# State outputs behind the chain, the output stage in two parts, and priority for three kinds of VectorE instruction, in an RWKV-7 and differential-attention trunk

## The chip, the cores and the metric

The kernel runs on one core of a Trainium2 chip. The metric is the device time of one execution in microseconds, lower is better. Engines are called as the profile calls them: PE is TensorE's matrix multiplier (PEld its weight loads), DVE is VectorE, ACT is ScalarE, POOL is GpSimd, SP is SyncE. L174 is line 174 of the kernel before.

## What is computed

Two layers over 2048 tokens of width 1024 in float32. The first is the one that matters here: a projection of the normalised input, RWKV-7 time mixing over 12 heads of 64 (a state matrix per head that is updated token by token), beside a small cross attention into 256 memory tokens. The second layer is differential attention. Cut to the recurrence:

```python
def step(state, inp):
    r_t, w_t, k_t, v_t, kk_t, a_t = inp
    sa = jnp.einsum('bhvk,bhk->bhv', state, -kk_t)
    state = (state * w_t[:, :, None, :]
             + sa[..., None] * (kk_t * a_t)[:, :, None, :]
             + v_t[..., None] * k_t[:, :, None, :])
    y_t = jnp.einsum('bhvk,bhk->bhv', state, r_t)
    return state, y_t
...
y = ((y - mean) * lax.rsqrt(var + LNX_EPS)).reshape(B, S, BR_W) * lnx_w + lnx_b
bonus = jnp.sum(r * k * r_k, axis=-1, keepdims=True) * v
return y + bonus.reshape(B, S, BR_W)
```

## The kernel before

Layer A is cut into 24 steps: two halves of the sequence, in each half six pairs of heads, for each pair two blocks of 512 tokens. A pair's weights serve both of its blocks. A step handles a block in chunks of 64 tokens: within a chunk the recurrence becomes small matrix products, and from chunk to chunk the state goes through a chain of eight links.

The methods of class Step are the stages of one step. p1 projects k, r and v (pj, three passes of 24 products at L174, 24 products for each) and mixes each with the token before (mix: an ACT copy with a scale, two DVE additions, and a copy of the last column, named carry, for the next block). Between k and r it takes a sum of squares per head over TensorE (pss, L335), which needs the mixed k (kx), its product kk on DVE and a square rn on ACT. p2 makes the Gram products (pg) and transposes; p3 and p3b invert the 64x64 triangular matrices of a chunk (DVE's recurrence itmp and Ti, transposes T and TT, and products inv, invz, invr on TensorE); p4 makes the products that turn a chunk into one affine map (atp, nvp, txp, mrp, and ch at L530). gate projects the SiLU gate (24 more pj).

p4b is the chain: for each of the eight chunks one product into ch (L541) reads the state before the chunk and one ACT instruction scales it into the next state (L542, S, and sb for the last). A link is this pair. The outputs yp take 32 products: 16 that need no state (L550) and 16 that read a chunk's state (L555, two for a chunk); in the profile each such product stands as two records. p5 is the output stage: statistics over a head (bn_stats, a few 128x8 operations on DVE, and two on ACT), two 128x512 operations on DVE (L574, L575), four transposes py on TensorE (L578), an ACT copy with the norm's weights, an addition, and the product with the gate on POOL, which also issues the store.

The kernel is written with tile pools; a scheduler sets each engine's order from priorities, which follow the order in which the code is written, and from its own estimate of when an instruction is ready. The loop over steps lets p2 and p3 of the next step stand ahead of p4b and p5 of this one, with p1 and gate of later steps as filler. All projections of layer A take turns in three PSUM banks (tag pj); the rest of layer A in three others, and ch in two of its own. On the engines the order is fixed then, and each engine runs its queue in that order.

A stretch, below, is the time from the first Gram product (pg) of one step to that of the next; there are 24. In stretch 3 and on, it holds the chain of the step before, the gate and the k projection of later steps, then pss, then 48 products for r and v. Weight halves are loaded by SP (wraw), copied by ACT (wh, L122) and split by POOL (wl, L123) once a pair, in turn with the projections that read the old ones.

Of the kernel before, what the change touches and what calls it, by code (L numbers as in the profile page):

```python
# [11 lines left out]
ALU = mybir.AluOpType  # L12
# [13 lines left out]
TB = 512  # L26
NC = TB // C
NJ = NC // 2
# [8 lines left out]
BIG = float(2.0 ** 60)  # L37
# [22 lines left out]
def hybrid_kernel(ctx, tc, S, HALF, x, mem, pv, cv, dist, postn, w_out, w_mkv, a_w, w2, a2, w_kv, b_w, out):  # L60
# [3 lines left out]
    mm = nc.tensor.matmul  # L64
    V = nc.vector
# [143 lines left out]
    def layer_a(ph):  # L209
# [17 lines left out]
        carry = pa.tile([P, 19], F32, name="carry")  # L227
# [25 lines left out]
        def PS(shape, name, tag="gm", bufs=3):  # L253
            if tag == "pj":
                return ppj.tile(shape, F32, name=name, tag="pj", bufs=3)
            return pps.tile(shape, F32, name=name, tag=tag, bufs=bufs)
# [17 lines left out]
        def mix(ps, col, o):  # L274
            m = pc("mu", col)
            A.activation(o, ps, AF.Copy, scale=omu[:, col:col + 1])
            V.scalar_tensor_tensor(out=o[:, 1:TB], in0=ps[:, 0:TB - 1], scalar=m, in1=o[:, 1:TB], op0=ALU.mult, op1=ALU.add)
            V.scalar_tensor_tensor(out=o[:, 0:1], in0=carry[:, col:col + 1], scalar=m, in1=o[:, 0:1], op0=ALU.mult, op1=ALU.add)
            V.tensor_copy(out=carry[:, col:col + 1], in_=ps[:, TB - 1:TB])

        def gate_silu(ps, g, eng=G_):
            A.activation(g, ps, AF.Copy)  # L282
            e = W([P, TB], "e_sil")
            A.activation(e, g, AF.Exp, scale=-1.0)
            V.tensor_scalar(out=e, in0=e, scalar1=BIG, scalar2=None, op0=ALU.min)
            A.activation(e, e, AF.Ln, bias=1.0)
            A.activation(e, e, AF.Exp, scale=-1.0)
            eng.tensor_tensor(out=g, in0=g, in1=e, op=ALU.mult)
            return g
# [13 lines left out]
        class Step:  # L303
# [5 lines left out]
            def p1(self):  # L309
                p, h, th, ws = self.p, self.h, self.th, self.ws  # L310
# [4 lines left out]
                for i, e in enumerate((cum[:, :, 1:65], asg.rearrange("p (c t) -> p c t", t=C))):  # L315
                    pl = PS([P, TB], "lr", "pj")
                    mm(pl, lhsT=lora[:, i], rhs=th[i], start=True, stop=False)
                    mm(pl, lhsT=lora[:, 2 + i], rhs=th[i], start=False, stop=True)
                    A.activation(e, pl.rearrange("p (c t) -> p c t", t=C), AF.Exp, bias=nwa[:, i * 6 + p:i * 6 + p + 1], scale=-1.0)
                    V.tensor_scalar(out=e, in0=e, scalar1=BIG, scalar2=None, op0=ALU.min)  # L320
                    A.activation(e, e, AF.Ln, bias=1.0)
                    A.activation(e, e, AF.Exp, scale=-1.0)
                kx = W([P, TB], "kx")
# [209 lines left out]
            def p4b(self):  # L533

                Gm, UV, PC, ch, MT, RT = self.Gm, self.UV, self.PC, self.ch, self.MT, self.RT
                hcs = (slice(0, 64), slice(64, 128))
                b = self.t0 // TB
                S = T([P, NC, C], "S", 1)
                st = [sb[self.p][:, b % 2]] + [S[:, c] for c in range(1, NC)] + [sb[self.p][:, 1 - b % 2]]
                for c in range(NC):  # L540
                    mm(ch[:, c, :], lhsT=MT[:, c, :], rhs=st[c], start=False, stop=True, skip_group_check=True)  # L541
                    A.activation(st[c + 1], ch[:, c, :], AF.Copy, scale=PC[:, c:c + 1])  # L542
                ys = self.ys = T([P, NJ, 2, C], "ys", 1)

                py = [PS([P, NJ, C], "yp") for hh in range(2)]
                for hh in range(2):
                    for j in range(NJ):
                        for e in range(2):
                            rr = hcs[e]
                            mm(py[hh][rr, j, :], lhsT=Gm[:, e, j, hh, rr], rhs=UV[:, 2 * j + e, hcs[hh]], start=j == 0, stop=False, skip_group_check=True)  # L550
                for j in range(NJ):
                    for e in range(2):
                        for hh in range(2):
                            c, rr = 2 * j + e, hcs[e]
                            mm(py[hh][rr, j, :], lhsT=RT[hcs[hh], c, :], rhs=st[c][hcs[hh]], start=False, stop=True, skip_group_check=True)  # L555
                for hh in range(2):
                    A.activation(ys[:, :, hh], py[hh], AF.Copy)

            def p5(self):
                p, ys, sil = self.p, self.ys, self.sil  # L560
                bs = T([P, 8, 6], "bs", 1)
                y8 = ys.rearrange("p j h v -> p (j h) v")
                for i in range(8):
# [9 lines left out]
                A.activation(sm[:, 3], sm[:, 3], AF.Exp, scale=-0.5)  # L573
                V.tensor_tensor(out=y8, in0=y8, in1=sm[:, 0, :, None].broadcast_to([P, 8, 64]), op=ALU.subtract)  # L574
                V.tensor_tensor(out=y8, in0=y8, in1=sm[:, 3, :, None].broadcast_to([P, 8, 64]), op=ALU.mult)  # L575
                py = PS([P, NJ, P], "py")
                for j in range(NJ):
                    nc.tensor.transpose(py[:, j, :], ys[:, j].rearrange("p h v -> p (h v)"), ident)  # L578
# [114 lines left out]
        for i in range(n):  # L693
# [10 lines left out]
            steps[i].p5()  # L704
            if i + 1 < n:
                steps[i + 1].p3b()
                steps[i + 1].p4()
            if i + 2 <= n:
                filler(i + 2)
            if i == n - 2:  # L710
# [613 lines left out]
```

## Time and profile before

| | |
|---|---|
| median of three runs | 3177.18 us (3177.15 to 3179.72) |
| the profiled execution's own time | 3178.13 us |
| its span in the trace | 3176.3 us |
| PE busy | 2965.9 us, 93% of the span |
| mean granted clock of TensorE | 0.970 |

The profile is of one execution. Its time is 0.95 us above the median and 1.8 us above its span. Busy shares are shares of the span; a busy PE is not one at its peak, since matmuls are pipelined and their ends are modelled. Layer A with its 24 stretches runs from 72 to some 1490 us of the span.

### The profile page before, as it was taken

What the parts mean: (1) busy time and instruction counts of PE and PEld (TensorE: products, weight loads), DVE (VectorE), ACT (ScalarE), POOL (GpSimd) and SP (SyncE); (2) the same over time, 40 slices, a digit from 0 to 9 for tenths busy, and PEclk for the clock granted to TensorE, in tenths of its full rate; (3) what the DMA queues carried; (4) which work ended last, traced back from release to release, by engine and by line L of the source; (5) the groups of instructions that cost most, each with busy time, mean ns of one, the idle gap of its engine ahead of it and who ended that gap; (6) DMA issues with size and microseconds to landing.
All of it is one profiled execution on the core that took longest, in us unless ns stands there. A gap on an engine that the chain in (4) does not pass through costs nothing.

```text
span 3176.3 us, 57448 instructions
## 1 busy us (share of the span) xinstructions
PE 2965.9 (93%) x22378; PEld 2401.6 (76%) x22378; DVE 1792.0 (56%) x4728; ACT 1508.2 (47%) x3318; POOL 873.6 (28%) x936
## 2 busy tenths in 40 slices
PE   6889999998789999998899999999999999998999
PEld 4667777776667777777677798898887787786777
DVE  6566767655656676764465311101108888887554
ACT  5535454444444544444455422313216777776343
POOL 3133433442134334431000222412312223222100
PEclk8999999998789999999999999999999999999999
DMA  3211000122110001103554523423454556533453
GB/s 118 80 30 36 28 23 26 35 77 79 36 33 28 23 26 33 38 25 86 164 145 126 155 80 99 118 83 87 117 158 110 114 112 120 116 80 108 121 156 115
DMA packets 266160, 265.45 MB, mean 84 GB/s; under 512 B 16832, under 2 KB 206656, under 8 KB 265760
## 3 DMA queue, kind: packets, MB, share of 16 engines
q1 hardware_dynamic: 237760, 195.31, 21.0%
q0 software_dynamic: 28128, 66.46, 10.3%
q8 instruction: 176, 2.88, 0.4%
q14 instruction: 96, 0.79, 0.1%
HBM read 180.45 MB, written 81.26 MB: 82 GB/s over the span
## 4 chain that ended last, share of the span: by engine, by line
PE 71%; DVE 13%; ACT 8%; issue 3%; DMA 3%; POOL 1%; SPq 1%; ACTq 0%; DVEq 0%; POOLq 0%
PE pj L174 28%; PE po L866 10%; PE o L1179 5%; PE vps L1042 4%; PE s L1138 3%; PE s L1139 2%; PE tr L1169 2%; DMA wraw<-in_a_w 2%; PE inv L446 2%; PE yp L555 1%; PE ch L541 1%; PE mo L805 1%; DVE E L1141 1%; PE mpt L798 1%; PE pss L335 1%
## 5 line engine op out<-in xcount | busy, mean ns | idle before, releaser
L174 PE MATMUL pj<-hhi,wh 128*128 128x512 f32 x928 | 396.3, 427 | 7.8 <-ACT sil L282 2.6
L174 PE MATMUL pj<-hhi,wl 128*128 128x512 f32 x928 | 379.4, 409 | 1.3 <-POOL wl L123 1.3
L174 PE MATMUL pj<-hlo,wh 128*128 128x512 f32 x928 | 373.9, 403 | 0.2 <-DVE hlo L149 0.2
L123 POOL TENSOR_TENSOR wl<-wraw,wh 128x512 fp32r<-128x512 f32 x168 | 220.0, 1320 | 431.5 <-ACT wh L122 378.0
L1141 DVE CUSTOM_DVE_ANT_0 E<-s,dist 128x512 f32<-128x512 f32 (+1 forms) x480 | 276.0, 604 | 35.2 <-PE s L1139 29.0
L174 PE MATMUL pj<-bh,wh 128*128 128x512 f32 x672 | 262.4, 391 | 0.0
L174 PE MATMUL pj<-bh,wl 128*128 128x512 f32 x672 | 262.3, 390 | 0.0
L174 PE MATMUL pj<-bl,wh 128*128 128x512 f32 x672 | 262.2, 390 | 0.0
L1146 ACT ACTIVATE E<-E,nm 128x1920 f32<-128x1920 f32 (+7 forms) x192 | 229.4, 1199 | 59.0 <-DVE nm L1144 58.6
L174 PEld LDWEIGHTS pj<-hhi,wh 128*128 128x128 f32 x928 | 179.2, 193 | 64.7 <-ACT sil L282 8.9
L122 ACT ACTIVATE wh<-wraw 128x512 fp32r<-128x512 f32 x168 | 105.2, 627 | 231.3 <-PE pj L174 143.6
L1179 PE MATMUL o<-th,vs 128*128 128x256 f32 (+1 forms) x864 | 210.9, 376 | 2.4 <-ACT th L1172 0.9
L174 PEld LDWEIGHTS pj<-hlo,wh 128*128 128x128 f32 x928 | 179.7, 194 | 41.7 <-issue 6.8
L174 PEld LDWEIGHTS pj<-hhi,wl 128*128 128x128 f32 x928 | 178.6, 192 | 42.0 <-POOL wl L123 2.2
L1138 PE MATMUL s<-ks,qd 128*128 128x512 f32 (+1 forms) x480 | 205.7, 432 | 2.2 <-DVE mx L1141 1.2
L1179 PEld LDWEIGHTS o<-th,vs 128*128 128x128 f32 x864 | 153.9, 189 | 38.5 <-ACT th L1172 19.2
L1139 PE MATMUL s<-ks,qd 128*128 128x512 f32 (+1 forms) x480 | 176.2, 373 | 0.0
L174 PEld LDWEIGHTS pj<-bh,wh 128*128 128x128 f32 x672 | 126.6, 188 | 26.3 <-DVE ot L877 0.3
L174 PEld LDWEIGHTS pj<-bh,wl 128*128 128x128 f32 x672 | 126.5, 188 | 26.3
L174 PEld LDWEIGHTS pj<-bl,wh 128*128 128x128 f32 x672 | 126.5, 188 | 25.9
L764 POOL DMA_DIRECT2D mq<-mq x64 | 33.3, 526 | 376.0 <-PE ms L783 368.3
L1172 ACT ACTIVATE th<-tr 128x512 f32<-128x512 f32 (+1 forms) x216 | 113.2, 568 | 44.2 <-PE tr L1169 43.8
(416 smaller groups left out, 7112.1 us busy)
## 6 DMA issues: line engine op xcount, KB each, us to landing
wraw<-in_a_w SPq DMA_DIRECT2D x126, 256.0 KB, 2.9
qd<-qd_d POOLq DMA_DIRECT2D x48, 512.0 KB, 7.0
mq<-mq POOLq DMA_DIRECT2D x64, 256.0 KB, 4.3
ks<-ks_d POOLq DMA_DIRECT2D x24, 512.0 KB, 7.2
yr<-y_dram SPq DMA_DIRECT2D x31, 384.0 KB, 5.0
xt<-in_x SPq DMA_DIRECT2D x16, 512.0 KB, 5.3
x_dram<-ot SPq DMA_DIRECT2D x16, 512.0 KB, 4.2
wraw<-in_b_w SPq DMA_DIRECT2D x32, 256.0 KB, 3.1
```

What stands on the lines that cost most here:

```text
L122: A.activation(hi[:, ks], raw, AF.Copy)
L123: eng.tensor_tensor(out=lo[:, ks], in0=raw, in1=hi[:, ks].bitcast(F32), op=ALU.subtract)
L174: mm(ps, lhsT=w[a_][:, k, wcol], rhs=h[b_][:, k, tsl], start=n == 0, stop=n == 3 * KT - 1)
L446: mm(pb[rows, j, hh, :], lhsT=lt[rows, j, hh, :], rhs=rt_[rows, j, hh, :], start=True, stop=True)
L866: mm(po[hf], lhsT=a_[:, k, :], rhs=b_[hf][:, k, :], start=k == i == 0, stop=k == KT - 1 and i == 2)
L1042: mm(ps[:, t, :], lhsT=hT[b][a_][:, k, tsl], rhs=w[b_][:, k, :], start=n == 0, stop=n == 3 * KT - 1)
L1138: mm(ps[:, f:f + w_], lhsT=qd[:, 0, c, qs], rhs=k_[:, c, 0:w_], start=True, stop=False)
L1139: mm(ps[:, f:f + w_], lhsT=qd[:, 1, c, qs], rhs=k_[:, c, 0:w_], start=False, stop=True)
L1141: V.tensor_tensor_reduce(out=e[:, kb * 512:kb * 512 + w], in0=ps[:, 0:w], in1=dt_[:, u0:u0 + w], scale=-SLOPES[h], scalar=3.0e38, op0=ALU. ...
L1146: A.activation(E[c][:, 0:nk], E[c][:, 0:nk], AF.Exp, bias=nm[:, c:c + 1], scale=-1.0, accum_out=nm[:, 2 + c:3 + c])
L1172: A.activation(th[:, 0:w], ps[:, 0:w], AF.Copy)
L1179: mm(po[:, oc], lhsT=vs[kt // 4][:, kt % 4, :], rhs=th[:, rc], start=n == 0, stop=n >= nmm - 2, skip_group_check=True)
```

## The change

Four edits, all of them in layer A. In p4b the 16 outputs that read a state (L555) get an edge that puts them behind the chain's last product in TensorE's order. p5 is cut in two: what follows L575, from the transposes py on, becomes p5b, which is called after the next step's p3b and ahead of its p4 (for the last step at the end). In mix, the three DVE instructions that read the projection's bank, and in p1 and gate_silu the min on DVE, are traced with high priority for the scheduler. No instruction is added or taken away: the count of each kind on each engine is the same.

```diff
         def mix(ps, col, o):
             m = pc("mu", col)
             A.activation(o, ps, AF.Copy, scale=omu[:, col:col + 1])
-            V.scalar_tensor_tensor(out=o[:, 1:TB], in0=ps[:, 0:TB - 1], scalar=m, in1=o[:, 1:TB], op0=ALU.mult, op1=ALU.add)
-            V.scalar_tensor_tensor(out=o[:, 0:1], in0=carry[:, col:col + 1], scalar=m, in1=o[:, 0:1], op0=ALU.mult, op1=ALU.add)
-            V.tensor_copy(out=carry[:, col:col + 1], in_=ps[:, TB - 1:TB])
+            with tc.high_priority():
+                V.scalar_tensor_tensor(out=o[:, 1:TB], in0=ps[:, 0:TB - 1], scalar=m, in1=o[:, 1:TB], op0=ALU.mult, op1=ALU.add)
+                V.scalar_tensor_tensor(out=o[:, 0:1], in0=carry[:, col:col + 1], scalar=m, in1=o[:, 0:1], op0=ALU.mult, op1=ALU.add)
+                V.tensor_copy(out=carry[:, col:col + 1], in_=ps[:, TB - 1:TB])
...
-            V.tensor_scalar(out=e, in0=e, scalar1=BIG, scalar2=None, op0=ALU.min)
+            with tc.high_priority():
+                V.tensor_scalar(out=e, in0=e, scalar1=BIG, scalar2=None, op0=ALU.min)
...
                 for c in range(NC):
-                    mm(ch[:, c, :], lhsT=MT[:, c, :], rhs=st[c], start=False, stop=True, skip_group_check=True)
+                    last = mm(ch[:, c, :], lhsT=MT[:, c, :], rhs=st[c], start=False, stop=True, skip_group_check=True)
...
-                for j in range(NJ):
-                    for e in range(2):
-                        for hh in range(2):
-                            c, rr = 2 * j + e, hcs[e]
-                            mm(py[hh][rr, j, :], lhsT=RT[hcs[hh], c, :], rhs=st[c][hcs[hh]], start=False, stop=True, skip_group_check=True)
+                with tc.issue_after(last.ins):
+                    for j in range(NJ):
+                        for e in range(2):
+                            for hh in range(2):
+                                c, rr = 2 * j + e, hcs[e]
+                                mm(py[hh][rr, j, :], lhsT=RT[hcs[hh], c, :], rhs=st[c][hcs[hh]], start=False, stop=True, skip_group_check=True)
...
+            def p5b(self):
+                p, ys, sil = self.p, self.ys, self.sil
                 py = PS([P, NJ, P], "py")
...
             if i + 1 < n:
                 steps[i + 1].p3b()
+                if True:
+                    steps[i].p5b()
                 steps[i + 1].p4()
+            if False or i + 1 == n:
+                steps[i].p5b()
```

What the scheduler makes of it shows at three places. First TensorE at a chain, in a stretch in the middle of the first half. Names are out<-in; ch<-sb and ch<-S are the chain's products, yp<-UV the outputs without a state, yp<-sb and yp<-S those with one, pj projections. Before:

```order
L385 MATMUL pvt<-cvt,vx 128x128 x4
L541 MATMUL ch<-sb_122,MT 128x64
L550 MATMUL yp<-UV,Gm 64x64 x16
L555 MATMUL yp<-sb_122,RT 64x64 x2
L541 MATMUL ch<-S,MT 128x64
L555 MATMUL yp<-S,RT 64x64 x2
L174 MATMUL pj<-hhi,wh 128x512
L174 MATMUL pj<-hlo,wh 128x512
L541 MATMUL ch<-S,MT 128x64
```

The same place in the changed kernel (its lines stand 2 to 7 lower):

```order
L388 MATMUL pvt<-cvt,vx 128x128 x4
L544 MATMUL ch<-sb_122,MT 128x64
L553 MATMUL yp<-UV,Gm 64x64 x16
L174 MATMUL pj<-hhi,wh 128x512
L544 MATMUL ch<-S,MT 128x64
L174 MATMUL pj<-hlo,wh 128x512
L174 MATMUL pj<-hhi,wl 128x512
L544 MATMUL ch<-S,MT 128x64
```

The outputs with a state are gone from between the links; they stand in one run of 16 behind the eighth. Between two links there are two projections now, where one and two took turns.

Second, TensorE ahead of pss, in every second stretch. Before, the chunk products ch<-UV are followed by pss at once:

```order
L519 MATMUL mrp<-BKT,Wn 64x64
L520 MATMUL mrp<-Gm,Wn 64x64
L530 MATMUL ch<-UV,BKT 64x64 x16
L335 MATMUL pss<-rn,cvt 128x512
L174 MATMUL pj<-hhi,wh 128x512
```

In the changed kernel nine products of the k projection and the first three links of the next step's chain come in between (the last of the nine and the links):

```order
L174 MATMUL pj<-hhi,wh 128x512
L174 MATMUL pj<-hlo,wh 128x512
L174 MATMUL pj<-hhi,wl 128x512
L544 MATMUL ch<-sb_122,MT 128x64
L544 MATMUL ch<-S,MT 128x64 x2
L338 MATMUL pss<-rn,cvt 128x512
```

The k projection ends there right ahead of the links and of pss, which needs what is made from it. It did end ahead of invr, a good deal earlier. Stretches 3, 5, 7, 9, 15, 17, 19, 21 and 23 have this form, and stretch 11 with two links; stretch 13 has it in both kernels, and stretch 14 had four links there before and none now. The stretches between (4, 6, 8 and so on) begin with what is left of the chain, five links.

Third, ACT at the same place in the changed kernel; kx is the mixed k, Pt and cum belong to the decay, S are the links' scalings, rn the square for pss:

```order
L122 ACTIVATE wh<-wraw 128x512
L276 ACTIVATE kx<-pj,omu 128x512
L331 ACTIVATE Pt<-cum 128x520
L545 ACTIVATE S<-ch,PC 128x64
L332 ACTIVATE cum<-cum 128x520
L545 ACTIVATE S<-ch,PC 128x64
L122 ACTIVATE wh<-wraw 128x512
L336 ACTIVATE rn<-kk 128x512
```

The two scalings and both weight halves stand among the instructions that pss waits for; before, no S stood between kx and rn in these stretches.

## Rows read from the trace of the kernel before

**Rows 1.** The page, part 1: busy time, share of the span, instructions.

```profile
PE 2965.9 (93%) x22378; PEld 2401.6 (76%) x22378; DVE 1792.0 (56%) x4728; ACT 1508.2 (47%) x3318; POOL 873.6 (28%) x936
```

**Rows 2.** Windows: length, busy PE, PEld, DVE, ACT, POOL, granted clock, DMA.

```profile
480.50:531.60 51.10, 47.06 (x539) 37.70 (x538) 33.48 (x93) 23.70 (x52) 19.96 (x20) 1.00 0.10 30
531.60:581.10 49.50, 46.96 (x537) 37.42 (x536) 36.35 (x93) 24.25 (x53) 20.19 (x20) 1.00 0.09 28
581.10:633.60 52.50, 48.58 (x536) 38.73 (x536) 33.59 (x93) 23.80 (x52) 19.89 (x20) 0.97 0.11 32
905.30:966.10 60.80, 52.81 (x541) 42.07 (x540) 36.55 (x93) 24.30 (x53) 19.12 (x19) 0.89 0.07 22
966.10:1014.90 48.80, 45.68 (x531) 35.82 (x530) 35.43 (x93) 22.72 (x49) 19.35 (x20) 1.00 0.09 28
```

**Rows 3.** Waits of PE from 431 to 581.1 us: total, times, longest.

```profile
PE py L578 <- DVE ys L575: 3.0, 3, 1.3
PE pg L371 <- DVE carry L279: 1.8, 2, 1.2
PE txp L504 <- ACT X L495: 1.5, 3, 0.5
```

**Rows 4.** Timeline of PE in a chain: start, duration, line, tiles, records.

```profile
234.19 1.15 PE L550 MATMUL yp<-UV,Gm 128*64 128x64 f32 x32
235.27 0.33 PE L555 MATMUL yp<-sb,RT 64*64 64x64 f32 x4
...
237.82 0.33 PE L541 MATMUL ch<-S,MT 128*128 128x64 f32 x2
238.08 0.33 PE L555 MATMUL yp<-S,RT 64*64 64x64 f32 x4
238.34 0.50 PE L174 MATMUL pj<-hhi,wh 128*128 128x512 f32 x1
238.68 0.39 PE L174 MATMUL pj<-hlo,wh 128*128 128x512 f32 x1
238.91 0.33 PE L541 MATMUL ch<-S,MT 128*128 128x64 f32 x2
...
241.98 0.33 PE L555 MATMUL yp<-S,RT 64*64 64x64 f32 x4
```

**Rows 5.** Timeline of ACT: a link's scaling in that chain, a weight copy after it.

```profile
238.18 0.31 ACT L542 ACTIVATE S<-ch,PC 128x64 f32<-128x64 f32 x1 [0.55 <-PE ch L541]
...
258.79 0.62 ACT L122 ACTIVATE wh<-wraw 128x512 fp32r<-128x512 f32 x1
```

**Rows 6.** Timeline of DVE: the first transpose of the inverse in that stretch.

```profile
245.61 1.07 DVE L427 STREAM_TRANSPOSE T<-X 128x512 f32<-128x512 f32 x1
```

**Rows 7.** Timeline of PE in stretch 13, links right ahead of pss.

```profile
886.20 0.33 PE L541 MATMUL ch<-sb,MT 128*128 128x64 f32 x2
888.16 0.43 PE L541 MATMUL ch<-S,MT 128*128 128x64 f32 x2 [1.63 <-ACT S L542]
889.00 0.69 PE L541 MATMUL ch<-S,MT 128*128 128x64 f32 x2 [0.41 <-ACT S L542]
891.07 2.07 PE L335 MATMUL pss<-rn,cvt 128*128 128x512 f32 x2 [1.38 <-ACT rn L333]
```

**Rows 8.** Timeline of ACT at the same place.

```profile
889.87 0.63 ACT L122 ACTIVATE wh<-wraw 128x512 fp32r<-128x512 f32 x1 [0.92 <-DMA wraw<-in_a_w]
890.40 0.61 ACT L333 ACTIVATE rn<-kk 128x512 f32<-128x512 f32 x1
```

**Rows 9.** Timeline of PE: pss in an ordinary stretch, and in stretch 14.

```profile
468.45 1.12 PE L335 MATMUL pss<-rn,cvt 128*128 128x512 f32 x2
...
947.40 0.33 PE L541 MATMUL ch<-sb,MT 128*128 128x64 f32 x2
951.27 2.08 PE L335 MATMUL pss<-rn,cvt 128*128 128x512 f32 x2
```

**Rows 10.** Timeline of ACT: a weight copy just ahead of the copy of v.

```profile
480.94 0.63 ACT L122 ACTIVATE wh<-wraw 128x512 fp32r<-128x512 f32 x1 [4.34 <-DMA wraw<-in_a_w]
```

More of the change, by code (lines that the diff above doesn't have):

```diff
@@ L319, in p1 @@
                     A.activation(e, pl.rearrange("p (c t) -> p c t", t=C), AF.Exp, bias=nwa[:, i * 6 + p:i * 6 + p + 1], scale=-1.0)
-                    V.tensor_scalar(out=e, in0=e, scalar1=BIG, scalar2=None, op0=ALU.min)
+                    with tc.high_priority():
+                        V.tensor_scalar(out=e, in0=e, scalar1=BIG, scalar2=None, op0=ALU.min)
                     A.activation(e, e, AF.Ln, bias=1.0)
@@ L559, in p5 @@
             def p5(self):
-                p, ys, sil = self.p, self.ys, self.sil
+                ys = self.ys
                 bs = T([P, 8, 6], "bs", 1)
```

## The prediction

> **What bounds the kernel now.** First the page: PE is busy for 93% of the span and no other engine above 56% [rows 1]. So only two things can make time: gaps on PE and a lower clock. Then the windows cut at the first Gram product of a step, which show layer A as a beat: a short stretch of 49.5 us follows a long one of 51.1 [rows 2]. PE's busy time is the same in both (46.96 and 47.06), so what differs is waiting; a short one has 2.5 us of it, a long one 4.0. Some long ones take 52.5 at a granted clock of 0.97 (the third row, one of four alike): 1.4 us for a part at 1.2 instead of 2.4 GHz. Next, what PE waits for [rows 3]: the transposes py for the output stage (3.0 us in three stretches, up to 1.3), the Gram products pg for a column copied on DVE (up to 1.2), txp for an ACT copy (0.5 in each). Last, a chain on PE's timeline [rows 4]: there the reader is to see no wait at all, but a pitch: a link's product, 0.26 us later the chunk's outputs, 0.26 later projections, and 0.34 between the first projection and the next where projections in a row follow at 0.23 (238.68 to 238.91).
>
> **Outputs behind the chain.** Eight times two outputs cost 8 x 0.26 = 2.08 us of PE between the links [rows 4]. In one run they should go as the 16 outputs without a state do, 32 records in 1.08 us (234.19 to 235.27). Gain 1.0 per step. Bounds: nothing, if products that read different states don't pack; 1.0 is the row of the same shape of output, and I take it. A link must still fit between: its scaling starts 0.36 us after the product (237.82 to 238.18), takes 0.31 [rows 5], so the next product could start after some 0.7, and the new pitch with two projections is 0.26 + 0.34 + 0.23 = 0.83. ACT doesn't bind. The statistics need all outputs, which end where they ended: before at 241.98 + 0.26, after at about 242.1, since the 13 projections in the chain are four more than now.
>
> **Output stage in two parts.** In a short stretch the wait for py (0.85, what is left of 3.0 beside 1.3, for two) goes, and three projections now stand ahead of txp and cover its 0.5. What is late next is the inverse: its first products stood behind py and now stand behind 11 projections and three lora products, 14 x 0.23 = 3.2 us after 242.1, at 245.4. They need transpose T, which starts at 245.61 and takes 1.07 [rows 6]; with two statistics and two small sums fewer ahead of it, some 0.5 earlier, so T ends near 246.1. PE waits 0.7 (none to 1.3). Net -0.65. In a long stretch py's 1.3 and most of txp's goes, 0.6 for T comes: -1.15 with what invz loses.
>
> **k projection, links and pss.** This is the part that costs. In a short stretch the 13 k products that ran while py was awaited are gone from there; nine end behind ch, directly ahead of three links and pss. pss needs kx on ACT, two additions and kk on DVE, then rn on ACT, and the links' scalings stand among these. Before, all of it lay under invr, atp, nvp, txp, mrp and ch. The trace has this very piece, in stretch 13 [rows 7]: from the first link at 886.20 to pss at 891.07 are 4.87 us, in which PE waits 1.63, 0.41 and 1.38. Of it 0.92 is ACT's wait for a weight half [rows 8]; in the ordinary stretch that half copy has no wait [rows 5], so I take 3.95. Stretch 14's piece, with four links, took 3.87 (947.40 to 951.27) [rows 9]. Bounds 3.9 and 4.9.
>
> TensorE's products stay in order, so the 48 projections behind pss wait too, and behind them the next pg.
>
> **A short stretch** changes by -1.0 - 0.65 + 3.95 = +2.3. **A long one** has three links fewer in its chain, each 0.26 and the 0.11 by which a projection is late after it: -1.1; with outputs and waits -1.0 - 1.1 - 1.15 = -3.25.
>
> **Priority on DVE** I cost at nothing: in the order, the carry copy still stands behind the first Gram mask, so pg's wait stays; the mins move by one or two DVE instructions under the projections.
>
> **The clock.** After both pieces of rows 7 and 9 pss itself took 2.07 and 2.08 instead of 1.12 [rows 7, 9]: 1.2 GHz. From pss to the next pg it then took 14.2 (891.07 to 905.3) and 14.8 us (951.27 to 966.1), where an ordinary stretch needs 12.05 (468.45 to 480.5) [rows 2, 9]. So the fall costs 1.4 (a long stretch with one) to 2.7. My stalls are as long as the shorter of the two; I take 1.8 for each of ten. Of that 0.5 is hidden: at the end of a short stretch the copy of v stands behind a weight half that comes at 480.94 [rows 10], 0.4 after pg has begun. And the four falls in long stretches follow pg's long wait, which shrinks when projections end later: -6. Together 10 x 1.3 - 6 = +7.
>
> The Trainium skill ("TensorE: Matmul & The Clock Gate", section "Part 1: The HAM clock gate") has the half rate come after an idle stretch; three products run in each stall, so by its words the clock might stay, and the sum be 7 us lower. The rows of stretches 13 and 14 show it fall though products ran.
>
> **Sum**, over layer A's stretches: eight short ones, 3 to 9 and 17 to 23, +18.4; the 11th with two links +1.6; the 15th starts from 48.8, so +3.0; nine long ones -29.25; the 14th loses its own piece and what the clock took after it, 3.87 + 2.7 and half of the outputs' gain, -7.1; the steps at the start and at the half's change (2, 12, 13), where prep work from DMA sets the pace, -1 (+-5). Without the clock -14.4, with it -7.4. The profiled execution took 3178.1, so 3170.7; the median lies 0.95 lower, which makes **3169.8**. A measurement can tell about 0.2%, 6.4 us, from no change.
>
> **Rivals.** (1) The clock stays up: the links' products and the nine dense projections ahead keep it. Against it, both pieces in the trace. -14.4 on the median: 3162.8. Chance 0.17. (2) Slower: the fall of the clock costs 2.7 at every stall and hides nowhere, and the long stretches keep theirs: 10 x 2.7 = 27 on -14.4, so 3189.8; with stalls of 4.87 on top 3199. Place: right behind the new links, ten times. It decides from 1.4 us a stall beyond the 3.95. For it: the only two examples cost 2.2 and 2.7. Against: they stand in disturbed stretches. Chance 0.2. (3) The freed waits only move: PE gets to the inverse sooner, and DVE, whose work is the same, makes it wait for T, TT and Ta by what py saved. Then -0.65 and -1.15 fall to a half, some +8: 3178, no change. For it: DVE's recurrence and transposes aren't touched. Chance 0.18.
>
> **Numbers.** The forecast keeps 0.45; its own range is 3163 to 3177. The range for all, 3154 to 3191, leaves out the dearest end of (2). Faster: 0.28 of the forecast, all of (1), 0.03 of (3): 0.48. Slower: (2) and a few of the rest, 0.25. Same 0.27.
>
> **What would show it.** In the profile after: 16 state outputs in about 1.1 us; no wait before py; a wait of PE for T before the first inv of 0.5 to 1; short stretches near 52 to 53.5 us with pss some 4 us behind the first early link, a granted clock under 1 in them; long ones near 47.5. Wrong would be: outputs that still take 2 us; links that wait for S in the chain; pss that follows the links within 2 us; or a changed second layer, whose order is the same.

## The result: slower, and the profile after

The changed kernel takes 3206.07 us (median of four runs, 3203.70 to 3208.33) against 3177.16 us, a ratio of 1.0094, 95% interval 1.0077 to 1.0112. The forecast was 3169.8 with a range up to 3191: wrong in sign and outside the range. The profiled execution took 3208.33 us, its span 3206.5, at a mean granted clock of 0.959. One of the four executions of e2, below, took 6079.53 us; it is left out of e2's median and ratio, and e2's trace, which is of it, isn't used.

The page of the changed kernel, part 1, says nearly what [rows 1] said: the same instructions, PE and DVE busy 10 us longer each (2976.0 and 1802.3). The difference is told by windows cut at the stretches (columns as in [rows 2]). First stretches 3 to 10, 11 to 15 and 16 to 23 as three blocks, of the kernel before:

```profile
228.10:633.60 405.50, 379.18 (x4289) 302.86 (x4288) 279.46 (x744) 191.98 (x420) 160.55 (x156) 0.99 0.10 29
633.60:1014.90 381.30, 332.46 (x2987) 261.31 (x2986) 219.73 (x575) 176.25 (x401) 125.50 (x120) 0.88 0.17 50
1014.90:1419.60 404.70, 379.23 (x4289) 302.63 (x4289) 279.49 (x744) 191.71 (x419) 158.65 (x156) 0.99 0.10 29
```

The same blocks of the changed kernel, and below them three short stretches and a long one (the last):

```profile
227.20:652.80 425.60, 388.33 (x4289) 301.79 (x4288) 284.73 (x744) 192.35 (x420) 157.07 (x156) 0.95 0.09 28
652.80:1027.60 374.80, 327.81 (x2993) 254.18 (x2992) 216.30 (x575) 177.31 (x405) 125.69 (x120) 0.89 0.18 52
1027.60:1450.90 423.30, 386.55 (x4291) 298.75 (x4290) 283.96 (x744) 192.13 (x420) 154.31 (x155) 0.95 0.09 27
...
441.20:493.00 51.80, 47.13 (x543) 36.39 (x542) 36.05 (x93) 25.04 (x56) 19.29 (x20) 1.00 0.09 27
545.10:598.50 53.40, 48.73 (x543) 37.25 (x542) 36.04 (x93) 25.14 (x57) 20.07 (x20) 0.97 0.10 28
1079.10:1133.50 54.40, 49.98 (x545) 38.22 (x544) 35.60 (x93) 25.19 (x57) 19.67 (x20) 0.94 0.10 30
1133.50:1184.90 51.40, 46.66 (x531) 36.48 (x530) 35.51 (x93) 22.91 (x49) 19.08 (x19) 0.97 0.08 25
```

The sixteen ordinary stretches lose 20.1 + 18.6 = 38.7 us, the block in the middle gains 6.5. In the ordinary ones the clock went from 0.99 to 0.95. What a fall costs is read from the three short stretches, which do the same: 51.8 at full clock, 53.4 with one fall, 54.4 with a longer one: 1.6 and 2.6. Of the eight short stretches three have the first kind of fall (3, 5 and 9), four the second (17, 19, 21 and 23) and stretch 7 none, though PE's waits in it are the same; what decides that, no run here shows.

Waits of PE in one short and one long stretch (1079.1 to 1185.5; columns as in [rows 3]):

```profile
PE inv L449 <- DVE X L432: 2.5, 1, 2.5
PE pg L374 <- DVE carry L280: 2.3, 2, 1.7
PE ch L544 <- ACT S L545: 2.0, 2, 1.6
PE inv L449 <- DVE T L430: 1.1, 1, 1.1
```

The waits for py and txp of [rows 3] are gone, as forecast. In their place stand the links (2.0) and the inverse's T (1.1) in the short stretch, and in the long one the inverse (2.5) and pg (1.7).

The outputs in one run, in the timeline of PE: from 1092.13 to the next projection at 1092.76.

```profile
1092.13 0.27 PE L559 MATMUL yp<-sb,RT 64*64 64x64 f32 x2
...
1092.76 0.50 PE L174 MATMUL pj<-hlo,wh 128*128 128x512 f32 x1
```

The piece ahead of pss, in the same view, where it answers to [rows 7]:

```profile
1115.06 0.33 PE L544 MATMUL ch<-sb,MT 128*128 128x64 f32 x2
1117.02 0.43 PE L544 MATMUL ch<-S,MT 128*128 128x64 f32 x2 [1.63 <-ACT S L545]
1117.86 0.69 PE L544 MATMUL ch<-S,MT 128*128 128x64 f32 x2 [0.41 <-ACT S L545]
1118.90 2.07 PE L338 MATMUL pss<-rn,cvt 128*128 128x512 f32 x2 [0.35 <-ACT rn L336]
```

From the first link to pss are 3.84 us, and the third link already runs at half rate (0.69 for 0.43). Windows around it, the last of them at the next pg's wait; the granted clock is the third number from the right:

```profile
1106.00:1117.58 11.58, 9.47 (x184) 7.90 (x179) 4.44 (x12) 6.17 (x17) 3.14 (x3) 1.00 0.07 24
1117.58:1124.41 6.83, 6.20 (x13) 4.21 (x14) 1.54 (x3) 2.73 (x6) 2.54 (x2) 0.50 0.27 77
1124.41:1133.40 8.99, 8.99 (x40) 7.21 (x39) 5.46 (x7) 1.78 (x4) 7.24 (x5) 1.00 0.19 55
1138.06:1141.47 3.41, 3.41 (x13) 2.53 (x13) 3.15 (x4) 1.19 (x2) 2.04 (x2) 0.50 0.25 70
```

Full rate, half rate behind the links' wait, full rate again under the projections, and half rate again behind pg's wait.

pg's wait itself. DVE at the start of that long stretch, and POOL beside it; below each, the same place before (from 480.50, [rows 2]):

```profile
1134.59 0.75 DVE L278 SCALAR_TENSOR_TENSOR vx<-pj,pvt,vx 128x511 f32<-128x511 f32 x1 [2.85 <-ACT vx L276]
1135.25 1.31 DVE L279 SCALAR_TENSOR_TENSOR vx<-carry,pvt,vx 128x1 f32<-128x1 f32 x1
1136.49 0.68 DVE L376 TENSOR_TENSOR Gm<-pg,cvt 128x512 f32<-128x512 f32 x1
...
482.85 0.21 DVE L278 SCALAR_TENSOR_TENSOR vx<-carry,pvt,vx 128x1 f32<-128x1 f32 x1
```

```profile
1134.05 2.50 POOL L123 TENSOR_TENSOR wl<-wraw,wh 128x512 fp32r<-128x512 f32 x2 [1.17 <-ACT wh L122]
...
481.65 1.27 POOL L123 TENSOR_TENSOR wl<-wraw,wh 128x512 fp32r<-128x512 f32 x1
483.07 1.27 POOL L123 TENSOR_TENSOR wl<-wraw,wh 128x512 fp32r<-128x512 f32 x1 [0.15 <-ACT wh L122]
```

One column takes 1.31 us where it usually takes 0.21, and ends when POOL's second weight split ends (1134.05 + 2.50). Before, the second half came late from DMA, the two splits stood apart (481.65 to 482.92, then 483.07), and the column went through at 482.85 in 0.21. In seven of the eight long stretches of stretches 3 to 10 and 16 to 23 the column is held so after the change, in none of them before. The eighth, stretch 8, follows the short stretch that had no fall (7): there the column takes 0.21 and pg waits 1.0. The Trainium skill ("SBUF — State Buffer", section "SBUF: two separate sides") has an exclusive lock on a port pair between POOL and a DVE instruction with two SBUF inputs, held for a whole instruction. The rows agree: the column reads carry and vx from SBUF and is held, while the addition ahead of it (1134.59), which reads one of its inputs from the projection's PSUM bank, takes the 0.75 that it takes everywhere.

And the inverse's wait in the long stretch, on DVE and POOL; the last two lines of the first are the long stretch before:

```profile
1150.87 0.68 DVE L578 TENSOR_TENSOR ys<-ys,sm 128x512 f32<-128x512 f32 x1
1151.66 0.69 DVE L579 TENSOR_TENSOR ys<-ys,sm 128x512 f32<-128x512 f32 x1
1152.27 1.27 DVE L423 TENSOR_TENSOR Ti<-Ti,itmp 128x15 f32<-128x15 f32 x1
1153.57 1.71 DVE L428 TENSOR_SCALAR X<-Ti,cvt 128x256 f32<-128x256 f32 x2
1155.32 1.04 DVE L430 STREAM_TRANSPOSE T<-X 128x512 f32<-128x512 f32 x1
...
497.97 0.17 DVE L420 TENSOR_TENSOR Ti<-Ti,itmp 128x15 f32<-128x15 f32 x1
498.21 0.73 DVE L425 TENSOR_SCALAR X<-Ti,cvt 128x256 f32<-128x256 f32 x2
```

```profile
1152.18 1.32 POOL L123 TENSOR_TENSOR wl<-wraw,wh 128x512 fp32r<-128x512 f32 x1 [4.13 <-PE lr L320]
...
1153.50 1.28 POOL L123 TENSOR_TENSOR wl<-wraw,wh 128x512 fp32r<-128x512 f32 x1
```

Here both operations on ys stand ahead of X and T, and two splits on POOL run beside the last step of the recurrence and X: Ti takes 1.27 instead of 0.17 and X 1.71 instead of 0.73, 2.1 us together. So it is in all eight ordinary long stretches after the change and in none before; in a short stretch no split runs there, and T comes ahead of ys. The inverse's wait is 2.5 in all eight; a fall follows it in four (4, 6, 8 and 10).

### The profile page after: what moved, and what is told of

It reads as the page before. It is cut to its first block, busy times and chain, and to the rows that moved or that the text cites. A ratio compares the mean times of both kernels' runs of the same rounds, so it can differ in the third digit from the quotient of the medians.

```text
span 3206.5 us, 57438 instructions
## 1 busy us (share of the span) xinstructions
PE 2976.0 (93%) x22378; PEld 2389.9 (75%) x22378; DVE 1802.3 (56%) x4728; ACT 1508.6 (47%) x3318; POOL 862.9 (27%) x936
## 4 chain that ended last, share of the span: by engine, by line
PE 73%; DVE 15%; ACT 7%; issue 3%; DMA 2%; POOL 0%; SPq 0%; ACTq 0%; DVEq 0%; POOLq 0%
PE pj L174 31%; PE po L877 10%; PE o L1190 5%; PE vps L1053 4%; PE s L1149 3%; PE s L1150 2%; PE tr L1180 2%; PE inv L449 2%; DVE Ti L423 2%; DVE itmp L421 1%; DVE Gm L376 1%; PE mo L816 1%; PE pss L338 1%; DVE E L1152 1%; PE mpt L809 1%
## 5 line engine op out<-in xcount | busy, mean ns | idle before, releaser
L174 PE MATMUL pj<-hhi,wh 128*128 128x512 f32 x928 | 403.2, 435 | 4.4 <-ACT wh L122 1.0
L174 PE MATMUL pj<-hlo,wh 128*128 128x512 f32 x928 | 383.8, 414 | 0.0
L174 PE MATMUL pj<-hhi,wl 128*128 128x512 f32 x928 | 378.7, 408 | 1.3 <-POOL wl L123 1.3
L174 PE MATMUL pj<-bh,wh 128*128 128x512 f32 x672 | 262.5, 391 | 0.0
L174 PE MATMUL pj<-bh,wl 128*128 128x512 f32 x672 | 262.3, 390 | 0.0
L174 PE MATMUL pj<-bl,wh 128*128 128x512 f32 x672 | 262.3, 390 | 0.0
L174 PEld LDWEIGHTS pj<-hhi,wh 128*128 128x128 f32 x928 | 183.7, 198 | 58.6 <-issue 8.3
L174 PEld LDWEIGHTS pj<-hlo,wh 128*128 128x128 f32 x928 | 182.3, 196 | 44.7 <-issue 8.8
L174 PEld LDWEIGHTS pj<-hhi,wl 128*128 128x128 f32 x928 | 182.5, 197 | 38.2 <-POOL wl L123 2.2
L174 PEld LDWEIGHTS pj<-bh,wh 128*128 128x128 f32 x672 | 126.6, 188 | 26.4 <-DVE ot L888 0.3
L174 PEld LDWEIGHTS pj<-bh,wl 128*128 128x128 f32 x672 | 126.4, 188 | 26.3
L174 PEld LDWEIGHTS pj<-bl,wh 128*128 128x128 f32 x672 | 126.6, 188 | 25.9
```

Of the source, the lines that this page charges most:

```text
L174: mm(ps, lhsT=w[a_][:, k, wcol], rhs=h[b_][:, k, tsl], start=n == 0, stop=n == 3 * KT - 1)
```

## The experiments

Ratios are to the kernel before, run beside them, with their 95% intervals.

| kernel | us, median | ratio |
|---|---|---|
| the change | 3206.1 | 1.0094 (1.0077 to 1.0112) |
| e1: split alone | 3197.8 | 1.0075 (1.006 to 1.009) |
| e2: outputs in a run alone | 3217.1 | 1.0139 (1.0123 to 1.0156) |
| e3: priority alone | 3192.9 | 1.0074 (1.0052 to 1.0095) |
| e4: run and priority | 3214.5 | 1.0127 (1.0112 to 1.0142) |
| e7: run and split | 3202.0 | 1.0081 (1.0064 to 1.0098) |
| e5: the change, pss later | 3151.4 | 0.9919 (0.9899 to 0.9938) |
| e6: run, split, pss later | 3163.1 | 0.9960 (0.9946 to 0.9975) |
| e8: split, pss later | 3165.6 | 0.9967 (0.9952 to 0.9982) |
| e12: before, pss later | 3176.8 | 0.9997 (0.9987 to 1.0006) |
| e11: the change, pss less late | 3162.4 | 0.9947 (0.9932 to 0.9962) |
| e9: the change, stall filled | 3176.1 | 0.9995 (0.9986 to 1.0005) |
| e10: the change, column on ACT | 3188.9 | 1.0034 (1.0019 to 1.0049) |
| e13: both of these | 3176.0 | 1.0002 (0.9991 to 1.0013) |
| e14: e5, column on ACT | 3145.9 | 0.9902 (0.9887 to 0.9917) |
| e15: e5, pg's wait filled | 3133.4 | 0.9862 (0.9848 to 0.9877) |
| e16: e15, column on ACT | 3132.6 | 0.9859 (0.9843 to 0.9876) |

**One edit at a time.** e1, the split, against before:

```diff
                V.tensor_tensor(out=y8, in0=y8, in1=sm[:, 3, :, None].broadcast_to([P, 8, 64]), op=ALU.mult)
+
+            def p5b(self):
...
                 steps[i + 1].p3b()
+                if True:
+                    steps[i].p5b()
                 steps[i + 1].p4()
+            if False or i + 1 == n:
+                steps[i].p5b()
```

> The output stage in two parts alone; outputs stay between the links, no priority. Theory (the split is what costs: in short stretches it brings the k projection and three links ahead of pss, and the clock falls there and at the next pg): the same order of links ahead of pss, so slower than before by at least the 29 us of the whole change, plus the 1 us per step that the outputs in a run would have given, some 20: 3205 to 3230, with falls of the clock in both kinds of stretch. Rival (the outputs in one run cost, because links that follow one another with two projections keep ACT and DVE late): within 10 us of before, clock 0.97.

e2, the run of outputs:

```diff
-                for j in range(NJ):
...
+                with tc.issue_after(last.ins):
+                    for j in range(NJ):
...
```

> The edge that puts the 16 outputs behind the chain alone; output stage in one part, no priority. Theory (the split costs, the run gains): faster than before by about 1 us a step, 3150 to 3160, no link ahead of pss, mean clock at or above 0.97. Rival (the run of outputs is what lowers the clock): 3190 to 3210, clock 0.96.

e3, the priority on the three kinds of DVE instruction:

```diff
-            V.scalar_tensor_tensor(out=o[:, 1:TB], in0=ps[:, 0:TB - 1], scalar=m, in1=o[:, 1:TB], op0=ALU.mult, op1=ALU.add)
...
+            with tc.high_priority():
+                V.scalar_tensor_tensor(out=o[:, 1:TB], in0=ps[:, 0:TB - 1], scalar=m, in1=o[:, 1:TB], op0=ALU.mult, op1=ALU.add)
...
```

> The priority on the three kinds of DVE instruction alone. Both theories: no change, 3170 to 3184. A third possibility (the priority makes the Gram masks late, and pg's wait of 1.7 us in long stretches is its doing): pg waits 1.7 here too, and 3190 or more.

e4, the change with the cut taken back:

```diff
-            def p5b(self):
-                p, ys, sil = self.p, self.ys, self.sil
...
-                if True:
-                    steps[i].p5b()
```

> The whole change without the cut of the output stage: outputs in a run, priority, p5 in one part. Theory: as the run alone, 3150 to 3162. Rival (the run or the priority cost): 3190 to 3210.

Of e1 and e2 the theory fell (the split costs less than the whole change, the run costs where it was to gain), and so did e1's rival; each edit alone makes the kernel slower, the run most. None of these kernels is the change less an edit, though: the scheduler lays all out anew, in e4 with pss ahead of txp, in e1 with seven products of k ahead of the links. What the run does is seen in e4, which holds it, over a long and a short stretch at full clock (1024.3 to 1076.2 to 1127.1):

```profile
PE py L582 <- DVE ys L579: 5.3, 2, 3.1
```

PE's busy time fell by 0.7 and 0.9 (46.32 and 46.05) against [rows 2], and py's wait rose to 2.2 and 3.1: in its order on DVE the small sums of the statistics start behind both transposes of the inverse (in another short stretch TT at 455.56, the first sm at 457.14), where before they started ahead of T. What TensorE saves it waits for, and the pair takes 102.8 us for 100.6. In e3 it is pg that waits 1.7, in seven of the eight long stretches, by the held column; five of the eight have a fall, as the one from 377.8 (53.2 us, clock 0.97). That is the third possibility named for it. The split alone has the links ahead of pss, and two neighbouring stretches without a fall show its price without the clock:

```profile
1276.60:1328.50 51.90, 47.91 (x543) 38.20 (x542) 35.17 (x93) 24.92 (x56) 19.22 (x20) 1.00 0.09 27
1328.50:1378.40 49.90, 45.85 (x533) 36.44 (x532) 34.20 (x93) 23.06 (x49) 20.18 (x20) 1.00 0.11 33
```

That is 101.8 for a pair where [rows 2] give 100.6: 1.2 a pair, some 10 us over eight pairs. In e1's trace the ordinary stretches lose 29.8 us (420.1 and 419.9 in two blocks) and the middle gains 14.8 (366.5), so the other 20 of the 29.8 are put down to the clock (an estimate).

e7, the change without the priority (the three edits with high_priority undone):

```diff
-            with tc.high_priority():
-                V.scalar_tensor_tensor(out=o[:, 1:TB], in0=ps[:, 0:TB - 1], scalar=m, in1=o[:, 1:TB], op0=ALU.mult, op1=ALU.add)
+            V.scalar_tensor_tensor(out=o[:, 1:TB], in0=ps[:, 0:TB - 1], scalar=m, in1=o[:, 1:TB], op0=ALU.mult, op1=ALU.add)
...
```

> The change without the priority: outputs in a run and the split, with the links ahead of pss (five products of k ahead of them instead of nine). Theory (stall and clock): as the whole change within 8 us, 3195 to 3212. Rival (the priority is what costs the rest): 3185 or less.

As the theory had it: within the whole change the priority makes no difference that can be told.

**The stall ahead of pss.** e5 is the change with pss traced behind nine products of r; the scheduler sets pss behind 15 of them, and no link comes ahead of it.

```diff
+                pr = PS([P, TB], "pj", "pj")
+                proj(pr, ws[1], h, slice(0, TB), part=(0, 9))
                 mm(pss, lhsT=bones, rhs=rn, start=True, stop=True)
...
-                mix(pj(ws[1], h), p, rx)
+                proj(pr, ws[1], h, slice(0, TB), part=(9, 24))
+                mix(pr, p, rx)
```

> The whole change, with pss put behind the first half of the r projection (in the order: 9 of k and 15 of r, then pss, then 33), so that no link comes ahead of it and TensorE has products while kx and rn are made. Theory now (the stall ahead of pss and the clock's fall right behind it are the larger part of the loss): no wait for S or rn, no fall at the ends of stretches, pairs of stretches near 100 us as before, 3165 to 3185. Rival (the loss sits in the waits that moved to pg and the inverse, 1.7 and 2.5 us in long stretches, and in the clock's fall behind pg's wait): still 3190 to 3205.

e6, e8 and e12 make the same edit without the priority, with the split alone, and in the kernel before; their diff is the one above.

> As the run before it, without the priority on DVE. If the priority costs by itself, 10 us or more below the kernel with it; if it is the weight splits on POOL that hold DVE's column instruction (1.31 us in the changed kernel where it took 0.21 before) whatever the priority, within 6 us of it.

> The split alone, with pss behind the first half of r; outputs between the links as before, no priority. Theory (of the split's 24 us the stall ahead of pss and the falls behind it are nearly all): at least 15 us below the split alone, 3170 to 3182. Rival (the split costs because the inverse then waits for DVE): 3190 to 3200.

> The kernel before with pss behind part of the r projection and nothing else of the change. Theory (there the place of pss cost nothing, since the k products ended early; only pg's wait can grow): 3174 to 3195. Rival (the later pss is worth 20 us or more in itself, and the change adds nothing to it): 3150 to 3162.

e5 is 55 us below the change, and below the theory's range too. Its short and long stretch, its waits over both, and its three blocks of stretches:

```profile
1034.90:1085.20 50.30, 45.89 (x537) 35.38 (x537) 37.96 (x94) 25.18 (x55) 19.98 (x21) 1.00 0.09 28
1085.20:1136.20 51.00, 48.83 (x538) 37.90 (x538) 35.98 (x93) 23.71 (x51) 18.73 (x20) 0.93 0.10 30
...
PE pg L378 <- DVE AR L363: 3.7, 3, 2.8
...
226.60:627.20 400.60, 374.41 (x4290) 290.35 (x4290) 295.54 (x744) 195.34 (x421) 155.32 (x157) 0.98 0.10 29
627.20:984.10 356.90, 315.63 (x2984) 247.07 (x2984) 223.67 (x576) 178.26 (x403) 125.65 (x121) 0.91 0.19 54
984.10:1387.60 403.50, 377.16 (x4290) 292.47 (x4290) 294.95 (x745) 195.26 (x419) 154.50 (x156) 0.97 0.10 29
```

No wait for S or rn, and no fall behind pss in the short stretches; ahead of the long ones pg now waits 2.8 for what follows pss on DVE, and in most of them the clock falls there. But the stall isn't all that went. In e5's long stretches no split on POOL runs beside Ti and X any more (0.16 and 0.45 for each half of X), and the inverse waits 0.4 instead of 2.5; how much of the 55 us is the stall's, e5 can't tell. e8 is 32 us below e1, more than its theory's 15, and there too the inverse's wait went.

Against the kernel before, the blocks say where e5 gains: 4.9 and 1.2 us in the ordinary stretches, 24.4 in the five in the middle. e12 has the time of the kernel before, but as a sum: its ordinary stretches take 9.9 us more (408.9 and 411.2) and the middle 12.4 less (368.9), most of it in stretch 14, where before links stood ahead of pss. So in the ordinary stretches of the kernel before pss's early place cost nothing, as the theory had it, and about half of what e5 gains in the middle the later pss gains by itself. The priority, nothing in e7, is worth 12 us in e5 against e6, which no theory had; why is open.

e11 sets pss between the two places, by an edge that holds the rest of r behind it:

```diff
+                pr = PS([P, TB], "pj", "pj")
+                proj(pr, ws[1], h, slice(0, TB), part=(0, 12))
+                last = mm(pss, lhsT=bones, rhs=rn, start=True, stop=True)
...
+                with tc.issue_after(last.ins):
+                    proj(pr, ws[1], h, slice(0, TB), part=(12, 24))
```

> The whole change with pss behind some 16 products of k and r and one link, the rest of r held behind pss (in the version that put pss behind 24 products, pg waits 2.8 us in long stretches for what follows pss on DVE and POOL). Theory (pss has a best place between a stall ahead of it and a late BK and AR behind it): pg's wait in long stretches falls to 2 or less, 3135 to 3150. Rival (any link or wait ahead of pss brings the stall and the clock's fall back): 3160 to 3180.

The time is the rival's, 11 us above e5, but not its mechanism: pss waits only 0.3, and no fall came back behind it. pg's wait fell to 2.5, not to 2 as the theory had it; AR comes of the part of r that is held back. The short stretches are 1.1 us longer than e5's at full clock, which is most of the 11; what in them costs it is open.

**The clock apart from the stall.** e9 puts four redundant products in front of the early links; edges hold the rest in place. In the ordinary stretches the order on TensorE, DVE and POOL is the change's; on ACT one weight copy moved, from ahead of kx to behind the links.

```diff
-                mm(pss, lhsT=bones, rhs=rn, start=True, stop=True)
...
+                if self.t0 // TB % NB == 1 and len(steps) > 3:
+                    for _ in range(4):
+                        lastd = mm(pss, lhsT=ws[0][0][:, 0], rhs=h[0][:, 0, 0:TB], start=True, stop=True)
+                    cur['dum'] = lastd
+                lastp = mm(pss, lhsT=bones, rhs=rn, start=True, stop=True)
...
```

> The changed kernel with four redundant 128x512 products (written to the bank of pss and overwritten by pss) between the nine k products and the early links, in every second stretch; the order of all else is the same. They add 0.9 us of work to TensorE inside a wait of 1.63. Theory (the clock falls there because TensorE waits, and the clock is most of the loss): falls at the ends of short stretches become fewer, and with each goes 1.6 to 2.6 us, so 3175 to 3195. Rival (the stall itself is the loss, or the clock does not follow TensorE's waits): 3200 to 3210, as many falls as before.

PE at the place in e9, and a short and a long stretch of it:

```profile
1204.44 1.07 PE L346 MATMUL pss<-hhi,wh 128*128 128x512 f32 x4
1205.35 0.33 PE L557 MATMUL ch<-sb,MT 128*128 128x64 f32 x2
1206.11 0.43 PE L557 MATMUL ch<-S,MT 128*128 128x64 f32 x2 [0.44 <-ACT S L558]
...
1207.99 1.12 PE L348 MATMUL pss<-rn,cvt 128*128 128x512 f32 x2 [0.60 <-ACT rn L341]
...
1168.50:1220.00 51.50, 48.03 (x549) 37.14 (x548) 36.03 (x93) 25.06 (x56) 19.33 (x20) 1.00 0.09 27
1220.00:1270.80 50.80, 46.66 (x533) 36.70 (x532) 34.15 (x93) 22.99 (x49) 20.15 (x20) 0.97 0.10 30
```

Work was added, pss still comes 3.55 us after the fill begins, and the kernel is 30 us faster, in the theory's range. In six of the eight short stretches pss now takes 1.12 and what follows it runs at full rate; a fall is left in two (3 and 5). The eight short stretches take 414.9 us together instead of 429.3: 14.4 less, of which a stall 0.3 shorter is 2.4 and the other 12.0 what the missing falls should give at 1.6 and 2.6. The long ones take 8.7 less (410.9 for 419.6): they are at half rate for less time, and the column is held in one of them instead of seven. So most of what e9 gains is the clock and what follows from its fall, not the stall's length. It is not a full return: e9's ordinary stretches still take 15.7 us more than before, and the middle (370.7) 10.6 less. The Trainium skill ("TensorE: Matmul & The Clock Gate", section "Part 1: The HAM clock gate") sets the rate by how busy TensorE has been; this run agrees. By the words from it in the prediction the three links might have kept the clock up; in seven of eight short stretches they did not; with four 128x512 products ahead of them it stayed up in six.

e10 takes the held column off DVE:

```diff
-                V.scalar_tensor_tensor(out=o[:, 0:1], in0=carry[:, col:col + 1], scalar=m, in1=o[:, 0:1], op0=ALU.mult, op1=ALU.add)
+                if 12 <= col < 18:
+                    A.activation(o[:, 0:1], carry[:, col:col + 1], AF.Identity, bias=o[:, 0:1], scale=m)
+                else:
+                    V.scalar_tensor_tensor(out=o[:, 0:1], in0=carry[:, col:col + 1], scalar=m, in1=o[:, 0:1], op0=ALU.mult, op1=ALU.add)
```

> The changed kernel with one instruction moved: mix's sum for the first column of v is one ACT instruction in place of the one on DVE. Theory (pg's wait of 1.71 us in long stretches is DVE's one-column instruction, held 1.31 us by the weight splits on POOL, and the fall behind it is that wait's): pg waits 1.0 or less, the falls at the starts of long stretches become fewer, 3180 to 3197. Rival (pg waits for the v projection's copy or for the masks anyway): pg still waits 1.5 or more, 3200 to 3210.

pg's waits in it, over a short stretch and a long one:

```profile
PE pg L377 <- DVE Gm L379: 1.0, 2, 0.5
```

pg waits 0.5 instead of 1.7 (the copy of carry also moved, ahead of the first mask), no fall is left at the start of a long stretch, and the long stretches last 50.4 us: the theory's case. A fall remains in each, behind the inverse's wait, which is 2.6: there the splits still hold Ti and X. e13 has both edits:

> The changed kernel with both: the four redundant products in the wait ahead of pss, and the first column of v on ACT. If the two causes are independent their gains add, 30 and 17 us on 3206: 3155 to 3165, and short stretches of 51.5 us with long ones of some 48.7 at full clock. If the second gain was only the clock's fall that followed the first, 3170 to 3178.

They don't add: the time is that of the second case. What stays is in the long stretch; a window of e13 behind the inverse's wait (its first product starts at 1127.73 after 2.57 us):

```profile
1128.83:1132.24 3.41, 3.41 (x25) 2.48 (x25) 1.06 (x2) 3.19 (x6) 1.48 (x3) 0.50 0.22 63
```

In seven of the eight long stretches the wait for DVE's T is followed by a fall, and a fall at the stall is left in four of the eight short ones, in spite of the fill; the two edits together only reach the kernel before. Filling this wait too, or moving the splits that lengthen it, with the order kept, wasn't tried.

**Beyond the change.** e14 is e5 with e10's edit.

> The whole change with pss later and the first column of v on ACT. There pg waits 2.8 us for AR of the r projection, which stands ahead of v on DVE, so the column is not what ends last: no change against 3151, 3145 to 3157. If the column's hold (0.57 us there) still delays the masks and the inverse: 3135 to 3145.

e15 is e5 with eight redundant products in pg's wait:

```diff
+                    if e == 0 and self.t0 // TB % NB == 1:
+                        for _ in range(8):
+                            mm(pgs[0].rearrange('p j t -> p (j t)'), lhsT=self.ws[2][0][:, 0], rhs=self.h[0][:, 0, 0:TB], start=True, stop=True)
```

> The whole change with pss later and eight redundant products (into pg's bank, overwritten by pg) ahead of pg in every second stretch, 1.8 us of work inside pg's wait of 2.8. If the clock's fall in long stretches comes from that wait, the falls there go, each 1.7 us or more: 3135 to 3147. If the fall has another source: 3150 to 3160.

e16 has both.

> The whole change with pss later, redundant products inside pg's wait, and the first column of v on ACT. If the column's hold costs by itself (it cost 0.1 to 0.3 us in a stretch where the clock stayed up), 3127 to 3133; if its gain of 5 us in the kernel without the fill was the clock's, 3132 to 3138.

A short and a long stretch of e15 (cut at the first product of the fill), and the fill:

```profile
1130.20:1177.50 47.30, 45.77 (x537) 35.53 (x538) 34.98 (x90) 23.91 (x53) 17.65 (x20) 1.00 0.10 29
1177.50:1229.00 51.50, 48.12 (x545) 36.72 (x544) 38.96 (x97) 24.70 (x53) 21.23 (x21) 1.00 0.10 30
...
1177.50 1.97 PE L377 MATMUL pg<-hhi,wh 128*128 128x512 f32 x8
```

The clock is 1.00 in both, as in all sixteen ordinary stretches of e15, and a pair takes 98.8 us. e15 is 18 us below e5, 1.6 below its own range, and 43 below the kernel before, the best of all with e16. e14's median is 5.5 us below e5's and e16's 0.8 below e15's, but in both pairs the runs overlap, and e16's 3132.6 lies in both of its ranges: whether the column costs anything here but the clock's fall isn't settled.

## Why the prediction was wrong

**Outputs in a run: right, mis-sized.** 0.63 us instead of the 1.08 taken from [rows 4], where the products are of another shape (128*64 against 64*64); the links' pitch is 0.84 (forecast 0.83), and ACT doesn't bind.

**Output stage: right in the short stretch, wrong in the long one.** py's and txp's waits are gone; T costs 1.1 in a short stretch (0.7, bound 1.3). "In a long stretch ... 0.6 for T comes" is the first step that failed: it is 2.5. I carried T's time over from a short stretch; in a long one TensorE comes without the three links that went to the stretch before, DVE has both ys operations ahead of T, and POOL's splits hold Ti and X for 2.1 us, which no term had. Without these 2.1 the wait would be near 0.4 (an estimate from the rows; no run moved the splits). That is rival (3), in the long stretches alone.

**The stall: right.** 3.84 against 3.95, and a short stretch at full clock takes 51.8, forecast 49.5 + 2.3. Two errors nearly cancel in it: the run saved 1.45 instead of 1.0, and T cost 0.4 more.

**Priority: right here** (e7), wrong as a rule: e3 alone costs 0.7%, e5 against e6 gains.

**The clock: the step that decided.** "The four falls in long stretches follow pg's long wait, which shrinks ...: -6" and "of that 0.5 is hidden". The four falls were to go; all eight ordinary long stretches have one or more, seven behind pg's wait, which grew from 1.2 to 1.7, for the column held by POOL's splits was not in the sum, and four behind the inverse's. And the weight half that was to hide 0.5 has long come: its copy no longer waits for DMA (1133.35, [3.71 <-PE pj L174]). With 1.6 to 2.6 us for a fall, three short stretches at 1.6 and four at 2.6 make 15 us. The long ones are at half rate for some 48 us (worked out from their lengths and clocks), and at the 0.43 us that a short stretch loses in each such us (1.6 for 3.4, 2.6 for 6.8) they make 21; before, four falls made 6. So of the 38.7 us about 30 are the clock (an estimate); the other 9 are eight short stretches at +2.3, less 1.2 in each long one instead of 3.25. Against the forecast of -7.4 the change measured +28.9; by these estimates the clock makes 23 us of that miss (30 for 7) and the long stretches' waits 16 (eight times 2.05), and what is left has the other sign.

So rival (2) came true, and was priced too low: the long stretches didn't keep their falls, they got more. Rival (1) had the clock stay up by the links' products; in seven of eight short stretches they didn't do it. e9 shows what most of it would have been worth, 30 us.

## What to carry to other kernels

A wait of TensorE of about 2 us is not priced by its length: look at the granted clock behind it, and at the next wait, which the same fall can bring on. Nor does its length tell whether a fall comes: the same waits had one in seven short stretches and none in the eighth. Where such a wait can't be removed, dense products into a bank that is overwritten anyway can pay for themselves; better, here, was to set a product that needs a long chain (pss) behind work that is ready. When a stage moves, follow the engine that was waited for in each kind of stretch, not in one, and look at what POOL will then do beside it: of DVE's instructions here the column, Ti and X took 1.0 to 1.1 us longer beside a weight split.

## What the hardware showed that I had not expected

Adding work made the kernel faster: four 128x512 products in nearly every second stretch took the changed kernel from 3206 to 3176 us, and eight took e5 from 3151 to 3133. A DVE instruction of one column took 1.31 us instead of 0.21 while POOL split weights. Sixteen outputs that contract over 64 rows (64*64 in the view) took 0.63 us in a row, where sixteen that contract over 128 (128*64) took 1.08 [rows 4].
